# Sums of |x| due four microseconds sooner in a planned matmul-tanh-multiply kernel

## The chip, the cores and the metric

The kernel runs on one core of one Trainium2 chip. The metric is the device time of one execution in microseconds, the median over runs. The core's engines are named as in the profile: PE (TensorE, the matmuls), PEld (its weight loads), DVE (VectorE), ACT (ScalarE), POOL (GpSimd, which here only issues the loads of x), SP (SyncE, which issues transposes and stores). A name with a q is an engine's queue of instructions that only wait or issue.

## What is computed

x has 16 batches of 512 rows and 1024 columns, w1 and w2 are 1024 by 768, all float32:

```python
def reference(x, w1, w2):
    y1 = np.matmul(x, w1)
    y2 = np.matmul(x, w2)
    return (np.tanh(y1) * y2).astype(np.float32)
```

The batches are flattened to 8192 rows, which are 64 row tiles of 128.

## The kernel before

**Row tiles and triples.** Row tiles 0 to 5 (the head) and 63 (the tail) are multiplied plainly. The 57 between are taken in 19 triples: triple i has row tiles 6+3i, 7+3i and 8+3i. A triple's x is seen as six blocks (three row tiles by two halves of the 1024 columns), the weights as six blocks too (two halves of the rows by three groups of 512 columns: a column block of w1, one of w2, and the rest of both). Instead of 18 block products the kernel makes 15 (`product`, L473, four matmuls of 128x512 each), from sums of x blocks (`x_sum`, L430, on VectorE, ten for a triple, named S) and sums of weight blocks (`w_sum`, L420, eleven, made once). The products gather in eight PSUM banks; copies and seeds (`c_copy`, L479, on ScalarE) and additions (`c_add`, L488, on VectorE) combine them, `c_tanh` (L491) and `c_mul` (L496) finish a triple's outputs. 60 of PE's matmuls make up a triple.

**How x comes in.** From row tile 4 on, a row tile passes three steps. The load L (`load_x`, L380) is a DMA that POOL issues, which casts x to float16 into an xh buffer. The transpose T (`transpose`, L383; from tile 6 on) is a DMA that SP issues, from xh to an xT buffer. The sum D (`abs_x`, L386) is one ScalarE instruction over xh which adds up |x| for a later test whether float16 was good enough (`flag_1` to `flag_5`; if not, `general_path` computes all again). So an xh buffer has two readers, T and D, and the next load into it waits for both. There are few xh buffers: three at first, and one more from row tiles 15, 18 and 21 on, so six (L370 to L376, `xh_user` names whose buffer a tile takes). With six, the first load of a group of three waits for the third row tile of the triple two groups back: load 24 waits for D20 and T20, load 25 for D18 and T18, load 26 for D19 and T19. The xT buffers are three triples' worth, and a transpose waits for the last reader of the buffer's row tile nine back.

**What sets the order.** Everything is an operation of a planner (class `Planner`, L78) with an engine and cost, a due time, and what it needs. `run` goes through them like a small simulation: on each engine it takes the operation that can start first, or an urgent one that is due sooner. Operations of the kinds in `SOON` ("S" and "D", L266) are not started more than 3.0 us ahead of their due time plus the lag of PE's fixed sequence. The order that comes out is written down engine by engine, with each engine's queue strictly in that order; the chip then runs each queue in order, and each instruction waits for its own operands. The planner's times have no other effect.

PE's order of products is fixed by `PE_ORDER` (L75). The transposes of a triple are grouped (L366 to L369): the third row tile first, then the first, then the second (T23, T21, T22), followed on SP by the three stores of the triple three before (L710 to L714). The loads are issued on POOL in the order of the row tiles, each behind the one before it.

**Due times.** The sum of row tile mt has its due time from the line that the change touches (L728): `ORIGIN - 12 + 4.33 * (mt - HEAD)`, where `ORIGIN` is 35.0, `HEAD` 6, and 4.33 is about a third of a triple, which is one row tile. The sums of the weights' 16 slices (`abs_w`, L386 also) have late due times (L550) and go where ScalarE has room.

Of the kernel before, what the change touches and what calls it, by code (L numbers as in the profile page):

```python
# [77 lines left out]
class Planner:  # L78
# [13 lines left out]
    def op(self, name, engines, due, needs, fn, *args, behind=(), issued=(), chains=(), xfer=0.0, latency=None, seeds=False):  # L92


        assert name not in self.ops, name
        self.ops[name] = dict(engines=engines, due=due, needs=[n for n in needs if n], behind=[n for n in behind if n], issued=[n for n in issued if n], fn=fn, args=args,
                              chains=chains, xfer=xfer, latency=latency, seeds=seeds)
        for c in chains:
            self.chains.setdefault(c, {"left": 0, "bank": None, "end": 0.0})["left"] += 1
# [133 lines left out]
def kernel(  # L233
# [26 lines left out]
    HEAD = 6  # L260
# [49 lines left out]
    op = plan.op  # L310
# [212 lines left out]
    ORIGIN = 35.0  # L523
# [136 lines left out]
    for i in range(TRIPLES):  # L660
# [6 lines left out]
        for o in C_OPS:  # L667
# [22 lines left out]
            mt = HEAD + 3 * i + r  # L690
# [24 lines left out]
    for mt in range(4, MT):  # L715
        j = xh_user[mt]
        prev = f"L{mt - 1}" if mt > 4 else "gate"
        op(f"L{mt}", {"pool": 0.55}, None, [], load_x, mt,
           issued=[prev], behind=[f"D{j}"] + [f"{u}{j}" for u in ("T", "PT") if f"{u}{j}" in plan.ops] if j else [], xfer=1.5)
        if mt < BY_PE:  # L720
            op(f"PT{mt}", {"pe": 0.5}, None, [f"L{mt}"], transpose_pe_h, mt, ("T", mt), chains=[("T", mt)])
            op(f"T{mt}", {"dve": 0.67, "act": 0.93}, None, [f"PT{mt}"], evacuate_h, mt, ("T", mt), chains=[("T", mt)])
            plan.ops[f"PT{mt}"]["due"] = 26 + 4 * (mt - 4)
        else:
            op(f"T{mt}", {"sp": 1.35}, None, [f"L{mt}"], transpose, mt,
               issued=([f"T{t_order[t_order.index(mt) - 1]}"] if mt > BY_PE else []),
               behind=xt_readers[mt - 3 * XT_BUFS] if mt >= 3 * XT_BUFS else [], xfer=1.45, latency=2.2)
        op(f"D{mt}", {"act": 1.05}, ORIGIN - 12 + 4.33 * (mt - HEAD), [f"L{mt}"], abs_x, mt)  # L728

    op("f1", {"dve": 0.3}, None, [], flag_1, behind=[f"D{mt}" for mt in range(MT)] + [f"aw{a}{k}" for a, t, k in slices])  # L730
    op("f2", {"dve": 0.2}, None, ["f1"], flag_2)
# [116 lines left out]
```

## Time and profile before

| what | value |
|---|---|
| median of 14 runs | 309.68 us (305.81 to 316.07) |
| the profiled execution, its own time | 309.64 us |
| its span, first to last instruction | 307.8 us |
| PE busy | 294.8 us (96%), 1418 matmuls |
| DVE busy | 238.7 us (78%) |
| ACT busy | 222.4 us (72%) |
| POOL busy (issuing loads) | 33.0 us (11%) |
| sums of \|x\|, `junk<-xh` x60 | 1054 ns each |
| loads of x, median from issue to landing | 5.4 us |
| transposes, median from issue to landing | 5.1 us |
| stores of 384 KB, median from issue to landing | 6.5 us |

The page gives each engine's busy time and, in 40 slices of the span (7.7 us each), its busy share in tenths. A row of a table by stages has the stretch, its length, then busy time and number of instructions of PE, PEld, DVE, ACT and POOL, the granted PE clock, the DMA share and GB/s. A line of waits has the engine and what it wrote, the one waited for, the sum, the number of times and the longest. A line of the timeline has the start, the length, and in brackets the idle time before it with what ended it. DMA queue q0 carries POOL's loads, q1 what SP issues (transposes and stores); its lines have packets, MB, and the packets' time as a share of the 16 DMA engines' stretch.

### The profile page before, as it was taken

Reading aid. Unit: us, or ns where it says so; the run is one execution under the profiler, and the core shown is the slowest. Engines: PE = TensorE matmul, PEld = TensorE weight load, DVE = VectorE, ACT = ScalarE, POOL = GpSimd, SP = SyncE. Lnnn points to the kernel's source line nnn. Section 1 sums busy time; section 2 is a strip of 40 time slices with the busy share of each in tenths; the row PEclk is TensorE's granted clock in tenths of the full one; section 3 lists DMA queues with packets and bytes.
Section 4 is the critical chain, followed back from the end, with each engine's and each line's share of the span. In section 5 each row is a group of like instructions: output and inputs, shape, how many; then the busy total and the mean of one; then the engine's idle time right before and its main releaser. Section 6 shows DMA issues by size and latency. Waiting matters only on the chain. (4 is left out here: it accounts for less than half of the span.)

```text
span 307.8 us, 4456 instructions
## 1 busy us (share of the span) xinstructions
PE 294.8 (96%) x1418; PEld 138.9 (45%) x1418; DVE 238.7 (78%) x497; ACT 222.4 (72%) x438; POOL 33.0 (11%) x67
## 2 busy tenths in 40 slices
PE   7899999999998699999999999999999999999994
PEld 4656544444343244444444444444444444444442
DVE  1208989977975688988889897898978989779754
ACT  3779999999583567596876868668696677774641
POOL 0030111022020102020210202102020120000000
PEclk9999999999999799999999999999999999999999
DMA  7999999599999994999999899999979989996143
GB/s 276 407 399 190 161 124 145 111 144 254 184 257 135 246 244 116 227 178 275 144 250 230 185 250 151 260 187 212 279 127 275 161 237 225 183 359 270 68 174 120
DMA packets 82584, 64.79 MB, mean 210 GB/s; under 512 B 63616, under 2 KB 64128, under 8 KB 82560
## 3 DMA queue, kind: packets, MB, share of 16 engines
q1 hardware_dynamic: 73344, 47.20, 58.1%
q0 software_dynamic: 8640, 15.73, 32.9%
q10 hardware_dynamic: 576, 1.57, 1.4%
q8 instruction: 11, 0.18, 0.2%
q14 instruction: 13, 0.11, 0.1%
HBM read 39.85 MB, written 25.17 MB: 211 GB/s over the span
## 5 line engine op out<-in xcount | busy, mean ns | idle before, releaser
L473 PE MATMUL bank<-b,s 128*128 128x512 f16 x608 | 143.1, 382 | 4.6 <-DVE s L488 4.2
L473 PEld LDWEIGHTS <-s 128*128 128x128 f16 x760 | 74.8, 98 | 96.2 <-issue 8.1
L479 ACT ACTIVATE s<-bank 128x512 f32<-128x512 f32 x95 | 55.9, 595 | 42.1 <-PE bank L473 40.6
L488 DVE TENSOR_TENSOR bank<-bank,s 128x512 f32<-128x512 f32 x95 | 65.6, 694 | 26.0 <-PE bank L473 11.9
L386 ACT ACTIVATE junk<-xh 128x1024 f16<-128x1024 f16 x60 | 63.2, 1054 | 0.2
L496 DVE TENSOR_TENSOR o<-o,bank 128x256 f32<-128x256 f32 (+1 forms) x114 | 60.1, 546 | 1.0 <-ACT o L491 0.9
L473 PEld LDWEIGHTS <-xT 128*128 128x128 f16 x380 | 37.0, 98 | 46.1 <-issue 2.2
L473 PE MATMUL bank<-b,xT 128*128 128x512 f16 x228 | 55.4, 379 | 0.0
L380 POOL DMA_DIRECT2D xh<-in_x_dram x60 | 32.2, 546 | 211.0 <-ACT junk L386 204.3
L473 PE MATMUL bank<-wh,xT 128*128 128x512 f16 x152 | 39.0, 379 | 1.0 <-ACT s L479 0.7
L445 PE MATMUL bank<-wh,xT 128*128 128x512 f16 (+1 forms) x208 | 38.8, 338 | 0.8 <-ACT xT L341 0.7
L473 PE MATMUL bank<-wh,s 128*128 128x512 f16 x152 | 39.2, 380 | 0.0
L491 ACT ACTIVATE o<-bank 128x256 f32<-128x256 f32 x76 | 31.5, 436 | 10.6 <-PE bank L473 6.6
L491 ACT ACTIVATE o<-s 128x512 f32<-128x512 f32 x38 | 23.8, 627 | 12.1 <-DVE s L488 11.4
L430 DVE TENSOR_TENSOR s<-s,xT 128x512 f16<-128x512 f16 x76 | 31.6, 416 | 0.2
L445 PEld LDWEIGHTS <-xT 128*128 128x128 f16 x208 | 20.0, 98 | 17.7 <-ACT xT L341 1.4
L479 ACT ACTIVATE bank<-bank 128x512 f32<-128x512 f32 x38 | 21.2, 576 | 5.0 <-PE bank L473 2.0
L488 DVE TENSOR_TENSOR bank<-s,bank 128x512 f32<-128x512 f32 x19 | 13.2, 692 | 12.0 <-ACT o L491 10.1
L343 DVE CAST wh<-w_f 128x768 f16<-128x768 f32 x8 | 4.5, 567 | 18.9 <-DMA w_f<-in_w_dram 18.9
L430 DVE TENSOR_TENSOR s<-xT,xT 128x512 f16<-128x512 f16 x38 | 15.9, 417 | 0.0
L430 DVE TENSOR_TENSOR s<-xT,s 128x512 f16<-128x512 f16 x38 | 15.8, 416 | 0.0
L386 ACT ACTIVATE junk<-wh 128x768 f16<-128x768 f16 x16 | 13.5, 845 | 0.2
(39 smaller groups left out, 120.7 us busy)
## 6 DMA issues: line engine op xcount, KB each, us to landing
out_dram<-o SPq DMA_DIRECT2D x60, 384.0 KB, 6.5
xh<-in_x_dram POOLq DMA_DIRECT2D x60, 256.0 KB, 5.4
w_f<-in_w_dram SPq DMA_DIRECT2D x12, 384.0 KB, 8.5
x_f<-in_x_dram SPq DMA_DIRECT2D x4, 512.0 KB, 7.7
w_f<-in_w_dram ACTq DMA_DIRECT2D x4, 384.0 KB, 7.3
out_dram<-o SPq DMA_DIRECT2D x4, 256.0 KB, 2.2
xT<-xh SPq DMA_TRANSPOSE x58, 5.1
out_dram<-o SPq DMA_DIRECT2D x4, 128.0 KB, 1.8
```

The costliest lines, as they stand in the source:

```text
L343: pin(engine[e].tensor_copy(dst, src))
L380: pin(nc.gpsimd.dma_start(xhs[mt], xf[mt]))
L386: pin(nc.scalar.activation(junk[:, :src.shape[-1]], src, ACT.Abs, scale=scale, accum_out=sums[:, column:column + 1]))
L430: pin(engine[e].tensor_tensor(ss[i, v], x_operand(i, a), x_operand(i, b), OP[how]))
L445: pin(nc.tensor.matmul(b, xts[mt][:, k, :], rhs, start=first, stop=k == KO - 1, skip_group_check=True))
L473: pin(nc.tensor.matmul(place(i, dst), x_operand(i, a)[:, k, :], w_rhs(b, k), start=begins and k == 0, stop=k == KH - 1, skip_group_check=T ...
L479: pin(nc.scalar.activation(d, place(i, src), ACT.Copy, scale=float(sign)))
L488: pin(nc.vector.tensor_tensor(d, a, b, ALU.add if signs == (1, 1) else ALU.subtract))
L491: pin(nc.scalar.activation(out_tile(HEAD + 3 * i + r)[:, lo:lo + n], place(i, src)[:, :n], ACT.Tanh, scale=float(sign)))
L496: pin(nc.vector.tensor_tensor(o, o, place(i, src)[:, at:at + n], ALU.mult))
```

## The change

The due time of a row tile's sum of |x| becomes 4 us sooner, for every row tile from 4 on. Nothing else in the code differs; what the planner makes of it, on all engines, follows from that number.

```diff
@@ -725,7 +725,7 @@
             op(f"T{mt}", {"sp": 1.35}, None, [f"L{mt}"], transpose, mt,
                issued=([f"T{t_order[t_order.index(mt) - 1]}"] if mt > BY_PE else []),
                behind=xt_readers[mt - 3 * XT_BUFS] if mt >= 3 * XT_BUFS else [], xfer=1.45, latency=2.2)
-        op(f"D{mt}", {"act": 1.05}, ORIGIN - 12 + 4.33 * (mt - HEAD), [f"L{mt}"], abs_x, mt)
+        op(f"D{mt}", {"act": 1.05}, ORIGIN - 16 + 4.33 * (mt - HEAD), [f"L{mt}"], abs_x, mt)
```

## The prediction

> **What bounds the kernel now.** I read the page's slices first, then the busy time by stages, the waits, and last the records around the one gap. In the slices TensorE (PE) is full except at the start, at the end and in slices 13 and 14 (92 to 108 us); the DMA row has two holes of its own, slice 8 (54 to 62 us) and slice 16 (115 to 123).
>
> ```profile
> PE   7899999999998699999999999999999999999994
> ...
> DMA  7999999599999994999999899999979989996143
> ```
>
> By stages, 120 to 300 us holds 836 matmuls in 180 us and nothing can be gained there: PE is the limit. The loss is in 97 to 107, where PE is busy 6.0 of 10 us and its granted clock is 0.83.
>
> ```profile
> 60.00:80.00 20.00, 19.32 (x90) 8.53 (x88) 16.36 (x37) 18.53 (x39) 4.24 (x8) 1.00 0.93 179
> 80.00:97.00 17.00, 16.72 (x79) 7.43 (x77) 13.95 (x30) 11.38 (x23) 1.59 (x3) 1.00 1.11 214
> 97.00:107.00 10.00, 6.00 (x21) 2.31 (x20) 4.84 (x10) 4.26 (x8) 0.73 (x2) 0.83 1.05 214
> ...
> 120.00:300.00 180.00, 179.66 (x836) 81.65 (x835) 151.71 (x326) 129.78 (x256) 18.05 (x34) 1.00 0.93 210
> ```
>
> The waits of 90 to 110 us name it: VectorE (DVE) waits 3.7 us, once, for a transposed x; PE then waits 4.0 us for VectorE, and the load queue (POOL) had stood 11.6 us up to 88.7 and 16.0 us up to 106.3, both times behind a sum of |x| (L386).
>
> ```profile
> POOL xh L380 <- ACT junk L386: 16.0, 1, 16.0
> ...
> PE bank L473 <- DVE s L488: 4.0, 1, 4.0
> DVE s L430 <- DMA xT<-xh: 3.7, 1, 3.7
> ```
>
> ```profile
> 102.82 3.43 PE L473 MATMUL bank<-b,s 128*128 128x512 f16 x8 [4.00 <-DVE s L488]
> 106.04 1.22 PE L473 MATMUL bank<-wh,s 128*128 128x512 f16 x4
> ```
>
> The late transpose is that of row tile 21 (T21), needed by the first x sum of triple 5. It was issued at 89.23 and landed at 100.53, 11.3 us later; transposes with the rings to themselves land in 3.1 to 3.8 us (T6 to T8). What was in its way were the loads of tiles 24 to 26, issued from 88.68. Their queue is q0, the transposes' q1. While both are full, q1 hardly moves:
>
> ```profile
> q0 software_dynamic: 328, 0.61, 89.3%
> q1 hardware_dynamic: 299, 0.07, 15.1%
> ```
>
> That is 91 to 96 us: 0.61 MB of loads and 0.07 MB of transposes. So a transpose that meets loads waits them out. Earlier the rings were empty from 60 to 63 us, because the load queue stood behind a sum that ended at 61.7:
>
> ```profile
> 61.86 2.12 POOL L380 DMA_DIRECT2D xh<-in_x_dram  x4 [10.80 <-ACT junk L386]
> 74.95 2.12 POOL L380 DMA_DIRECT2D xh<-in_x_dram  x4 [10.97 <-ACT junk L386]
> 88.68 1.59 POOL L380 DMA_DIRECT2D xh<-in_x_dram  x3 [11.61 <-ACT junk L386]
> ```
>
> **What the Trainium skill says.** "DMA: Bandwidth & Descriptors", Queues, rings and completion order: each DMA engine goes round between the queues that have work, a packet at a time. The trace agrees in kind; the shares above (89 to 15) show that a turn of q0 is worth far more time. The same page, Issuing engines are not separate DMA queues: what GpSimd, SP and ScalarE issue runs on the same 16 DMA engines. The trace agrees: three loads land in 7.5 us alone (121.29 to 128.76) and took 10.6 with stores and transposes in flight (88.68 to 99.26). "TensorE: Matmul & The Clock Gate", What's actually happening: an idle PE falls to half its clock and recovers only after a busy window. Here 4.0 idle us were followed by products of 1.5 and 1.7 us instead of 0.86.
>
> **The change, part by part.** No instruction is added or removed. The order listing gives the sums of |x| about one row tile sooner in ScalarE's order, from tile 8 on, with the weight sums spread around them; a few x sums and products move on VectorE; PE's order is the same but for seven entries of the last triple; loads and transposes keep their order, some stores swap. A sum costs ScalarE about 1.15 us (1.05 and its 0.19 read, overlapping by 0.1), before as after: ScalarE's total stays.
>
> What moves is the release of the load queue, which waits in order: each group of loads stands behind the sum (and the transpose) of the buffer's last user. Followed through with durations of the trace:
> - Sum 8 now runs right after sum 7 (ends 31.9), so it ends near 33.1 instead of 37.8. Load 11 then waits only for T8 (landed 35.02): issued near 35.2 instead of 38.21, 3 us sooner; T11, loads 14 and 15 follow by 2.5 to 3.
> - Sum 14 moves ahead of two seeds, a copy, two tanh and two weight sums, to right after the copy that the trace has at 52.6 (its place there, with sums 12 and 13 ahead of it, is near 54.4). It ends near 55.6 instead of 61.5. Loads 16 to 19 start near 56 instead of 61.86, into the hole of 60 to 63.
> - Sum 17 moves ahead of a group of copies and tanh, from 73.53 to about 67: loads 20 to 23 near 68.5 instead of 74.95.
> - Sum 20 moves from 87.25 to about 81.7 (after the tanh that ends at 80.8 and one weight sum): loads 24 to 26 near 83 instead of 88.68, 5.7 us sooner. Alone they flow at 0.83 tile a us after 1.5 us of start: done near 88 to 89.5, the stores of 85 to 86.7 beside them.
> - T23, T21, T22 stand on SP behind three stores that wait for the last outputs of triple 1 (VectorE, to 84.1). They move only to 85.2, 86.5 and 89.1. With loads done at 89.5 and 1.1 us for each transpose (their rate alone in the records of 104 to 106 us), T21 lands between 92 and 95. It is needed at 96.9 in the trace's frame, or some 2 us sooner, as the order now has this x sum earlier on VectorE.
>
> So the stall goes, possibly with a rest. Its worth: the product before it starts at 97.79, the fourth after at 107.09: 9.30 us for four products of 0.863, that is 9.30 - 3.45 = 5.85, slow clock included. What is late next are small gaps, 0.18, 0.85, 0.43 and 0.38 us (at 58.4, 78.4, 91.8, 117.8), where PE waits on ScalarE or VectorE; fewer weight sums stand in a row at 68 to 71, so I count half of their 1.84, 0.9, as gone.
>
> What it may cost: sums 12 and 13 now stand ahead of the copies that products at 52.2 and 55.6 wait for. The copy at 50.63 came from a ScalarE that had idled 0.48 before it; with 1.15 us put ahead of it, it starts near 51.3 and ends near 51.8, and its product starts at 52.16: covered by 0.3, less the signal. Nothing if loads 12 and 13 have landed, up to 1 us if the sum must wait for its load with copies queued behind it, and not below nothing: I take 0.3. For a rest at T21, between nothing and 3 us, I take 0.7, since its landing spans 3 us and its need 2.
>
> Sum, against the profiled execution's own 309.64 us (span 307.8 and 1.8 around it; the median of 14 is 309.68): 309.64 - 5.85 - 0.9 + 0.3 + 0.7 = 303.9.
>
> **The rivals.** *A rest of the stall.* The loads come earlier, but with stores beside them flow at half rate, and T21 meets their last tile; half the stall stays: 303.9 + 3 = 306.9. For it: T21 is only 1.5 to 3 us sooner on SP. Against: the loads are 5.7 sooner.
> *It does nothing.* The sums were late for want of ScalarE, not by order: between 40 and 80 us it is busy 37.2 of 40. Then the loads don't move and the time is 309.6. Against: the sums pass work that isn't due, weight sums above all.
> *Slower: the collision moves to another transpose, in every triple.* After 120 us the loads (34.0 of the frame, tile 33: 134.04) meet the triple's second transpose (T31: 135.29 to 143.06, 7.8 us), which has 0.7 to 2.3 us to spare. The third sum of a triple moves by 6.3 to 6.5, so loads start near 127.6 and flow to 134.5, over T32 and T30. T30 would land near 138 instead of 135.65; its x sum starts at 139.99. Spare 2 us: covered. If two or more us go in the mixing (the loads of 91 to 97 ran at 0.45 tile a us), PE loses about 1 us in each of 13 triples: 303.9 + 13 = 317. It decides from a landing more than 4.3 us later than before; the spare of those first transposes was 1.5 to 4.3 us.
>
> **How the numbers follow.** Stall gone: 0.64, 302 to 305.5. Rest: 0.16, 305.5 to 308. Nothing: 0.07. Slower: 0.13. The range runs from all gaps gone (309.64 - 5.85 - 1.84 = 302.0) to the end of the rest's case, 308.0, and holds 0.80. This kernel's measurement tells about 0.5% (1.5 us) from no change: faster 0.80, same 0.07, slower 0.13.
>
> **What would show it.** Right: no VectorE wait over 1 us for xT<-xh between 85 and 110, PE at clock 1.00 there, loads 16, 20 and 24 issued near 56, 68.5 and 83, the DMA hole at 60 to 63 filled, and 836 matmuls per 180 us kept. Wrong: loads that move by less than 3 us, T21 in flight over 8 us, or waits of VectorE for the first transpose of a triple, again and again after 120.

## The result, and the profile after

| | before | after |
|---|---|---|
| median of all executions | 309.49 us (47, 305.36 to 316.58) | 305.34 us (10, 302.70 to 309.75) |
| profiled execution, its own time | 309.64 us | 303.98 us |
| its span | 307.8 us | 302.1 us |

The change makes the kernel faster, by 1.3%: ratio 0.987 [0.9835, 0.9905]. Ratios, here and below, are made from the executions within 1.5% of each kernel's fastest, medians from all of them, so that for a kernel whose times scatter widely the ratio flatters and the median beside it says more. The forecast, 303.9 us, was made against the profiled execution, and the profiled execution after takes 303.98. That hit is partly luck, as the sum below shows; the medians are 4.15 us apart, where 5.7 was forecast.

In the page's slices of after, PE's hole in slices 13 and 14 is gone, and the DMA row has 8 and 9 in slices 8 and 16, where it had 5 and 4. PE has a small new dent in slice 17 (121 to 128 us):

```profile
PE   8999999999999999899999999999999999999995
...
DMA  7999999899999999999999999999999999595143
```

By stages (same columns as before), 97 to 107 us has PE busy throughout, at full clock. After 120 us the last row is new: before, the same stretch held 766 matmuls and 165.00 us of PE; now 753 and 163.21. Thirteen matmuls of 0.216 us are 2.8 us lost where before had lost nothing.

```profile
60.00:80.00 20.00, 20.00 (x94) 9.05 (x93) 17.48 (x39) 17.75 (x39) 2.12 (x4) 1.00 1.09 206
80.00:97.00 17.00, 17.00 (x80) 7.73 (x79) 14.77 (x32) 12.77 (x26) 2.88 (x6) 1.00 1.19 249
97.00:107.00 10.00, 10.00 (x49) 4.49 (x47) 8.24 (x19) 8.61 (x18) 0.30 (x1) 1.00 1.11 98
```

```profile
120.00:285.00 165.00, 163.21 (x753) 73.38 (x752) 140.86 (x302) 115.51 (x232) 16.36 (x31) 1.00 1.02 215
```

The load queue (POOL, timeline of after) starts each group about six microseconds sooner than before (61.86, 74.95 and 88.68 there):

```profile
55.58 2.12 POOL L380 DMA_DIRECT2D xh<-in_x_dram  x4 [9.59 <-ACT junk L386]
68.74 2.12 POOL L380 DMA_DIRECT2D xh<-in_x_dram  x4 [11.05 <-ACT junk L386]
82.60 1.59 POOL L380 DMA_DIRECT2D xh<-in_x_dram  x3 [11.74 <-ACT junk L386]
```

The waits of 90 to 110 us name neither PE nor VectorE for a transposed x any more. The load queue still waits there, for a sum (9.6 us) and now also for transposes (10.7 us at the longest): it is released by whichever of an xh buffer's two readers comes last.

```profile
POOL xh L380 <- DMA xT<-xh: 13.1, 3, 10.7
POOL xh L380 <- ACT junk L386: 9.6, 1, 9.6
```

What the prediction did not see is on SP's queue. Before:

```profile
79.84 5.16 SPq L383 DMA_TRANSPOSE xT<-xh  x3
85.09 1.61 SPq L439 DMA_DIRECT2D out_dram<-o  x3
86.80 7.73 SPq L383 DMA_TRANSPOSE xT<-xh  x3
```

After:

```profile
74.30 5.33 SPq L383 DMA_TRANSPOSE xT<-xh  x3
79.72 1.60 SPq L439 DMA_DIRECT2D out_dram<-o  x3
81.43 9.24 SPq L383 DMA_TRANSPOSE xT<-xh  x3
```

The first row of each begins with T20, the third with T23; T21 is the second of the third row. T20 is issued when its load lands: load 20 landed at 79.82 before, at 74.28 after. T18 and T19, the three stores and then T23 and T21 follow at once, one behind the other. So the earlier loads moved T21 as well, from 89.23 to 83.80, nearly as far as they moved load 24 (88.68 to 82.60). They still meet: T21 was in flight 9.38 us (11.30 before). But it lands at 93.18 instead of 100.53, and the x sum that needs it starts at 93.43. The meeting is not avoided; it is over in time.

After 120 us VectorE waits four times for a first transpose, as that of a triple's first row tile is called here (T27, T36, T48, T54). PE loses 1.2 us after two of these waits (0.6 to 0.9 us idle, the rest in slower products) and 0.6 after a third. The timeline of after, VectorE and then PE:

```profile
121.64 0.43 DVE L430 TENSOR_TENSOR s<-xT 128x512 f16<-128x512 f16 x1 [1.29 <-DMA xT<-xh]
158.25 0.43 DVE L430 TENSOR_TENSOR s<-xT 128x512 f16<-128x512 f16 x1 [0.79 <-DMA xT<-xh]
...
210.91 0.43 DVE L430 TENSOR_TENSOR s<-xT 128x512 f16<-128x512 f16 x1 [1.66 <-DMA xT<-xh]
...
238.00 0.43 DVE L430 TENSOR_TENSOR s<-xT 128x512 f16<-128x512 f16 x1 [2.55 <-DMA xT<-xh]
```

```profile
122.73 1.02 PE L473 MATMUL bank<-b,s 128*128 128x512 f16 x4 [0.68 <-DVE bank L488]
...
239.09 2.98 PE L473 MATMUL bank<-b,s 128*128 128x512 f16 x12 [0.47 <-DVE bank L488]
```

### The profile page after: what moved, and what is told of

It is laid out like the page before. It is cut to its first block, busy times and chain, and to the rows that moved or that the text cites. A ratio compares the mean times of both kernels' runs of the same rounds, so it can differ in the third digit from the quotient of the medians.

```text
span 302.1 us, 4460 instructions
## 1 busy us (share of the span) xinstructions
PE 294.0 (97%) x1418; PEld 139.1 (46%) x1418; DVE 240.3 (80%) x497; ACT 220.0 (73%) x438; POOL 33.0 (11%) x67
## 5 line engine op out<-in xcount | busy, mean ns | idle before, releaser
L479 ACT ACTIVATE s<-bank 128x512 f32<-128x512 f32 x95 | 55.0, 596 | 35.3 <-PE bank L473 35.1
L496 DVE TENSOR_TENSOR o<-o,bank 128x256 f32<-128x256 f32 (+1 forms) x114 | 60.8, 547 | 2.6 <-ACT o L491 2.1
L491 ACT ACTIVATE o<-bank 128x256 f32<-128x256 f32 x76 | 32.3, 436 | 17.1 <-DVE bank L488 14.4
L386 ACT ACTIVATE junk<-wh 128x768 f16<-128x768 f16 x16 | 13.5, 845 | 0.2
```

The costliest lines, as they stand in the source:

```text
L386: pin(nc.scalar.activation(junk[:, :src.shape[-1]], src, ACT.Abs, scale=scale, accum_out=sums[:, column:column + 1]))
L479: pin(nc.scalar.activation(d, place(i, src), ACT.Copy, scale=float(sign)))
L491: pin(nc.scalar.activation(out_tile(HEAD + 3 * i + r)[:, lo:lo + n], place(i, src)[:, :n], ACT.Tanh, scale=float(sign)))
L496: pin(nc.vector.tensor_tensor(o, o, place(i, src)[:, at:at + n], ALU.mult))
```

## The experiments

My theory after the result: the stall at 98 us went because the load queue is released sooner by a few sums, and its price is that later loads meet first transposes. The rivals: the new order on ScalarE or VectorE did it by itself; one load's release (load 24) is enough; the gain is in the later due times. Each diff is against the kernel before, line 728, unless another is named; the number that is changed is the 12.

**Four sums only (e1).** Sums 8, 14, 17 and 20 alone are due four microseconds sooner.

```diff
-ORIGIN - 12 + 4.33 * (mt - HEAD)
+ORIGIN - (16 if mt in (8, 14, 17, 20) else 12) + 4.33 * (mt - HEAD)
```

> Only the sums of row tiles 8, 14, 17 and 20 are due 4 us sooner, the other 56 stay as before. Theory 'loads' (the gain is the earlier release of loads 11 to 26, so that T21 no longer meets loads 24 to 26): the whole gain, 303 to 305.5 us, load 24 issued near 83, no VectorE wait over 1 us for a transposed x between 85 and 110; and after 120 us the loads meet each triple's second transpose as before, so no late first transposes. Rival 'ScalarE order' (the gain is that copies no longer queue behind crowded sums): four sums of 60 bring little, 308 to 310 us.

Measured: median 307.03 us (six executions, in two groups: 302.56, 302.71 and 306.90 to 309.95), before 309.08 beside it; ratio 0.986 [0.9776, 0.9943]. The profiled execution took 302.71 us. T21 went out at 83.91 and landed at 94.24, and there is no stall at 98. Four sums of 60 take the stall away. The four slower executions were not profiled; by the median the gain is 2 us, half of the change's.

**The late sums only (e2).** Sums from row tile 24 on, which the change moves also, without the early ones.

```diff
+ORIGIN - (16 if mt > 23 else 12) + 4.33 * (mt - HEAD)
```

> The sums of row tiles 24 and later are due 4 us sooner, those up to 23 stay as before. Theory 'loads': no gain, 308.5 to 311 us, the stall near 98 to 106 with T21 in flight about 11 us is still there, and the first transposes of later triples are late as in the changed kernel. Rival 'ScalarE order': part of the gain, 305 to 308 us.

Measured: median 313.65 us (310.85 to 317.15); ratio 1.0106 [1.0048, 1.0164]. This half of the change by itself makes the kernel slower, by about 1%. Its profiled execution, 317.15 us, is the longest of the six and overstates the size: the stall at 98 is there (PE idle 4.18), and VectorE's waits for a transposed x have grown from 3.7 us, once, to the following.

```profile
DVE s L430 <- DMA xT<-xh: 14.7, 6, 3.9
```

**Loads 24 to 26 held back (e3).** All sums stay as before; before load 24 GpSimd copies one element of T22's result, so that the loads start only when T22 has landed, the last of T23, T21 and T22 on SP. This takes the meeting away from the other side.

```diff
+    def gate_x(e, mt):
+        pin(nc.gpsimd.tensor_copy(held, xts[mt][:, 0, :2].bitcast(f32)))
...
+        if mt == 24:
+            op("gate_x", {"pool": 0.2}, None, ["T22"], gate_x, 22, issued=[prev])
+            prev = "gate_x"
```

> The sums stay as before; GpSimd reads one element of row tile 22's transposed x before it issues load 24, so loads 24 to 26 wait until T22 has landed. Theory 'loads': with nothing in its way T21 lands near 93 to 95 instead of 100.5, the stall at 98 goes, 303.5 to 306 us, though these loads are issued about 8 us later than before, near 97; what follows may be late (T24 to T26), which would take 1 to 2 us back. Rival 'ScalarE order': 309 us or more, since no sum has moved.

Measured: median 303.69 us (302.61 to 311.76, seven); ratio 0.9803 [0.9752, 0.9854]. In its profiled execution (310.13 us) the loads start at 97.40, and T21, issued at 90.42, later than in any other kernel of the table below, lands 5.4 us later at 95.86.

```profile
96.89 0.18 POOL L520 COPY held<-xT 128x1 f32<-128x1 f32 x1 [20.02 <-DMA xT<-xh]
97.40 1.59 POOL L380 DMA_DIRECT2D xh<-in_x_dram  x3 [0.33 <-issue]
```

PE idles 0.2 us there instead of 4.0. By lines and tile names the trace has the instructions of ScalarE and PE in the order of before from end to end, and those of VectorE up to 103 us. So the meeting caused the stall, and the rival of a new order on ScalarE or VectorE falls. What this execution lost, it lost at 128 us: behind the loads held back T27 went out late (116.43) and met loads 30 to 32 (115.20 to 125.56), 9.9 us in flight:

```profile
128.00 5.28 PE L473 MATMUL bank<-b,s 128*128 128x512 f16 x12 [3.96 <-DVE bank L488]
```

**Loads that do not wait for sums (e4).** From row tile 6 on the sum of |x| reads xT instead of xh (the range test then sums the same values, grouped otherwise), so that an xh buffer has one reader, the transpose.

```diff
-        abs_sum(e, (xfs if mt in xfs else xhs)[mt], mt)
+        abs_sum(e, xts[mt].rearrange("p k m -> p (k m)") if mt >= BY_PE else (xfs if mt in xfs else xhs)[mt], mt)
...
-           issued=[prev], behind=[f"D{j}"] + [f"{u}{j}" for u in ("T", "PT") if f"{u}{j}" in plan.ops] if j else [], xfer=1.5)
+           issued=[prev], behind=[f"{u}{j}" for u in ("T", "PT") if f"{u}{j}" in plan.ops] if j else [], xfer=1.5)
...
-        op(f"D{mt}", {"act": 1.05}, ORIGIN - 12 + 4.33 * (mt - HEAD), [f"L{mt}"], abs_x, mt)
+        op(f"D{mt}", {"act": 1.05}, ORIGIN - 12 + 4.33 * (mt - HEAD), [f"T{mt}" if mt >= BY_PE else f"L{mt}"], abs_x, mt)
+        if mt >= BY_PE:
+            xt_readers[mt].append(f"D{mt}")
```

> From row tile 6 on the sums of |x| read the transposed x instead of the cast x, with the old due times: the same number of elements a partition, but sums over other elements, so the range test tests other sums. A load then waits for the transpose of its buffer's last user alone. Theory 'loads': load 24 is issued near 82 to 86, T21 lands by 96, 302.5 to 306 us. Rival 'ScalarE order': sums come later than before (they wait for the transposes), 309 to 313 us.

Measured: median 314.30 us (304.26 to 319.58, six), too scattered for a ratio. It is inconclusive as a test of the release, for it makes a new wait: a sum now stands on ScalarE's queue behind its transpose, and the copies behind it wait too. In the profiled execution (307.68 us) the stall at 98 is gone (T21 landed at 91.65), but PE waits 3.8 us for such copies:

```profile
PE bank L473 <- ACT s L479: 3.8, 2, 2.2
```

**Sum 20 only (e8).** The sum that releases load 24, without the three before it in the chain.

```diff
+ORIGIN - (16 if mt == 20 else 12) + 4.33 * (mt - HEAD)
```

> Only the sum of row tile 20 is due 4 us sooner. Theory 'loads': it alone releases loads 24 to 26, so these are issued near 83 instead of 88.7 and are out of the way when T21 (issued near 89 as before) flows; the stall at 98 goes or shrinks to under 2 us and the fastest executions take 303 to 305 us. Rival 'backlog' (the loads 11 to 23, all sooner, are what lets T21 in): the stall stays, 308 to 310 us.

Measured: median 310.50 us (22 executions, 305.93 to 312.51), before 309.25 (43); ratio 0.999 [0.9958, 1.0022]: no gain. Load 24 was released earlier, but only to 85.07, since it then waited for T20 (landed 84.51), the buffer's other reader. T21 did not move at all (89.20), because load 20, which heads SP's queue, did not. The earlier loads met T23, the transpose ahead of it (14.0 us in flight), and the stall grew:

```profile
103.59 3.57 PE L473 MATMUL bank<-b,s 128*128 128x512 f16 x8 [5.37 <-DVE s L488]
```

The profiled executions side by side show what decides (microseconds; the x sum is the first of triple 5, the last column the longest wait of PE between 85 and 115):

| kernel | load 20 landed | T21 issued | load 24 issued | T21 landed | x sum starts | PE idle |
|---|---|---|---|---|---|---|
| before | 79.82 | 89.23 | 88.68 | 100.53 | 100.55 | 4.0 |
| after | 74.28 | 83.80 | 82.60 | 93.18 | 93.43 | none |
| e1, four sums | 74.52 | 83.91 | 83.44 | 94.24 | 94.27 | none |
| e2, late sums | 79.44 | 89.65 | 88.63 | 100.64 | 100.67 | 4.2 |
| e3, loads held | 80.88 | 90.42 | 97.40 | 95.86 | 96.57 | 0.3 |
| e8, sum 20 | 79.41 | 89.20 | 85.07 | 101.89 | 101.92 | 5.4 |

Either T21 goes out near 84 and may take ten microseconds, or it goes out near 90 and must not meet the loads. What the first 118 us gain is also much the same each time: the product that starts at 117.83 before starts 7.4 to 8.0 us sooner in the profiled execution of every kernel with the four sums sooner (after, e1 and e5, e6, e7, e11, e12 below), 6.1 sooner in e3, 0.3 in e2, and 0.7 later in e8. The scatter between the kernels that have the gain comes after that.

**Later due times for the rest (e5, e6, e9).** If early sums help up to row tile 20 and hurt after it, the late ones should be due later than before. e5 has the four sums and, from row tile 23 on, 9 in place of 12; e6 the same with 6; e9 the 9 without the four sums.

```diff
+ORIGIN - (16 if mt in (8, 14, 17, 20) else 9 if mt > 22 else 12) + 4.33 * (mt - HEAD)
```

> Sums 8, 14, 17 and 20 are due 4 us sooner as in the four-sums kernel, and those of row tiles 23 and later 3 us later than before. Theory 'loads': after 100 us the loads of a triple are then issued about 1.3 us later against PE, after its second transpose has begun to flow; that transpose lands 3.5 to 6 us after its issue instead of 6 to 8, its x sum has 3 us or more to spare, and the executions with a second stall (near 307 to 310 us in the four-sums kernel) become rare: median 302.5 to 304.5. Rival 'chance' (the second stall has nothing to do with which transpose the loads meet): median 305 to 308 with the same two groups of times.

Measured for e5: median 301.45 us, five of six executions between 301.31 and 302.38, one of 310.51; ratio 0.9741 [0.9708, 0.9774]. In the profiled one (301.41 us) no transpose between 110 and 250 us takes over 6.4 us (12.6 in after), and PE has hardly a gap:

```profile
120.00:296.00 176.00, 175.52 (x821) 80.06 (x819) 149.17 (x317) 123.80 (x247) 16.46 (x31) 1.00 0.90 212
```

> As the kernel before it in this call, but the sums of row tiles 23 and later are due 6 us later than before. Theory 'loads': loads are issued about 4.3 us later against PE, second transposes land within 4 us; the first and third transposes of the next triple now wait for later loads and land 3 to 4 us later than in the four-sums kernel, with 1 to 3 us to spare: median 302.5 to 305. If their spare is used up, PE waits for VectorE in many triples, 308 us or more. Rival 'chance': 305 to 308 as above.

Measured for e6: median 312.07 us (21 executions from 303.54 to 316.27 and one of 446.33), slower than before beside it (309.25); the ratio, 0.9885 [0.9822, 0.9947], counts only three of them and says little. Three microseconds more were too many: VectorE waits 10.6 us for transposes and PE 3.6 us for one of ScalarE's copies.

> The sums of row tiles 23 and later are due 3 us later than before, the head's sums stay as before. Theory 'two places' (the stall at 98 us comes from the head's load releases, the later losses from where loads meet transposes): the stall at 98 to 106 stays whole, 308 to 310 us. Rival 'the later due times are the gain' of the kernel that made both changes: 302 to 305 us.

Measured for e9: median 313.85 us (22, 308.37 to 325.84); ratio 1.0044 [1.0005, 1.0082]. The stall at 98 stays, but not whole as expected (T21 issued at 89.01, landed at 99.01, PE idle 2.8): the product of 117.83 starts 3.6 us sooner than in before, though up to 104 us its ScalarE, VectorE and PE have the order of before, by lines and tile names. So the stall itself differs in size from one execution to another. Later due times are not the gain by themselves.

**The same kernels again (e7, e12), and a mixture (e11).** e7 is the changed kernel unaltered, e12 is e5 unaltered. e11 takes the change up to row tile 22 and 9 from there on.

```diff
+ORIGIN - (16 if mt < 23 else 9) + 4.33 * (mt - HEAD)
```

> The changed kernel once more, unaltered, on the same chip as the others of this call. Theory 'loads': 303 to 306 us; first transposes of some triples (in flight 8 to 13 us where they meet loads) have almost nothing to spare, and PE loses 1 to 4 us in pieces after 120 us, not at one place. Rival 'it loses nothing after 120': all executions within 1 us of each other at 302.5 to 303.5.

Measured for e7: median 306.13 us (302.39 to 312.33, six); ratio 0.9819 [0.9769, 0.9869]. The gain repeats. The profiled execution took 306.46 us, again with no stall at 98 (T21 issued 84.32, landed 92.94) and again with losses after 120, about 5.4 us this time.

> The changed kernel with the sums of row tiles 23 and later due 3 us later than before instead of 4 us sooner; the head's sums as the change has them. Theory 'two places': the change's gain without its loss after 120 us, 301 to 302.5 us in most executions, no VectorE wait for a first transpose after 120. Rival 'four sums' (the other early sums of the head cost something): 303 to 305.

Measured for e11: median 308.35 us (22 executions, 301.03 to 315.45), before 309.53 beside it; ratio 0.9793 [0.9746, 0.9841]. Only four executions took 301.03 to 301.52 us, as was expected of most; the others lost 3 to 14. In the profiled one (308.94) PE idles 5.9 us at one place, 230 us, behind T51, which was 10.7 us in flight.

> The kernel with four head sums sooner and the sums of row tiles 23 and later 3 us later than before, unaltered, once more. Its six executions lay at 301.3 to 302.4 but for one at 310.5; the like kernel with all the head's sums sooner lay between 301 and 315 over 22 executions. Theory 'chance' (both kernels lose 4 to 10 us whenever one meeting of loads and transposes sets off others, and six executions were too few to see it): a third or more of the executions lie over 304 us, median 302.5 to 308. Rival 'four sums are safer' (moving only the sums that release loads keeps clear of it): at least four in five lie under 303 us, median 301.3 to 302.

Measured for e12: median 307.25 us (302.54, 302.68, 305.70, 308.79, 310.32, 316.32), before 308.92 beside it; ratio 0.9838 [0.9768, 0.9907]. So e5's five executions within 1.1 us of each other were good luck. The profiled execution (308.79) has T21 in time as e5 had, but T43 (11.0 us in flight) and T45 (8.4) late around 190 to 203 us, with 4.7 us idle of PE behind them:

```profile
DVE s L430 <- DMA xT<-xh: 9.1, 4, 6.0
```

One and the same program thus meets or misses at a late transpose from one execution to the next. No version here beats the changed kernel reliably.

**The meeting by itself (e10).** A kernel of its own, which computes nothing of the reference and writes zeros: six rounds of six transposes alone and then six with three loads of the same size and cast started beside them. GpSimd copies one element of each result, so that the next set begins after the last has landed.

```python
for r in range(6):
    s = r % 2
    transpose(s, 0)
    transpose(s, 3)
    gate(6)
    transpose(s, 0)
    transpose(s, 3)
    load(1 - s, r + 1)
    gate(6)
```

> Computes nothing of the reference: it only casts in row tiles by threes, transposes them, and fills the output with zeros. Six times over, six transposes flow alone, then six flow while three loads of other row tiles are issued. Theory 'loads': alone each transpose takes 1.1 to 1.3 us of the rings in a row; those that meet the loads hardly move until the loads have landed, so the last of them land 4 us or more later than without loads, and while both flow the transposes' queue moves under a fifth of its own rate. Rival 'fair shares': both queues slow down by half, the last transposes land about 2 to 4 us later and the loads take twice their time.

Measured, in one execution of 201.05 us. First all transposes (L38), then all loads (L34), with the time from issue to landing:

```profile
L38 SPq DMA_TRANSPOSE xT<-xh x72: 1232/1280/4211, 5.0 to 131.4; - x72
...
DMA to landing us min/median/max: 3.1/3.4/9.7
```

```profile
DMA to landing us min/median/max: 3.8/6.3/8.4
```

Alone nearly all transposes land in 3.1 to 3.5 us. In each round the first two of the second six, issued ahead of the loads, still land so. The third and fourth meet the loads: they take 7.9 to 9.7 us and land at least 0.5 us after the last load; the fifth takes 4.8 to 5.9. The queues while both are full (18.5 to 22 us; packets, MB, share):

```profile
q0 software_dynamic: 274, 0.51, 86.0%
q1 hardware_dynamic: 292, 0.07, 14.9%
```

These are the kernel's own shares of 91 to 96 us (89 to 15) with no store and no matmul near: the loads alone do it. With the engines to itself (13 to 18 us) the transposes' queue moved 0.93 MB in 5 us. The packets say how: 274 to 292, nearly one for one. That agrees with the Trainium skill ("DMA: Bandwidth & Descriptors", Queues, rings and completion order), which says that a DMA engine goes round its queues packet by packet, if the trace's packets are those that the page means. But a load's packet carries 1.9 KB (0.51 MB by 274) and a transpose's 0.24 KB (0.07 by 292), and so of eight parts moved the loads get seven.

## Why the prediction was right, and where it was not

The lead of after over before, read as the start of the same product in the one trace minus that in the other, adds the sum up term by term:

| where (time in before) | lead afterwards, us | change | the prediction's term |
|---|---|---|---|
| first products, 38 | 0.38 | +0.38 | none |
| product at 54.7 | 0.20 | -0.18 | sums ahead of copies, -0.3 |
| small gaps, 58 to 92 | 1.81 | +1.61 | half of the gaps, +0.9 |
| the stall, 98 to 107 | 7.66 | +5.85 | +5.85 |
| gap at 118 | 8.04 | +0.38 | in the +0.9 |
| 122 to 247 | 5.10 | -2.94 | covered, nothing |
| outputs after the last products | 5.7 (span) | +0.6 | none |

- **The stall** was worth what it was said to be, 5.85 us, and it went by the chain that was followed: sum 8 ended at 32.73 (33.1 predicted), load 11 started at 35.47 (35.2), load 16 at 55.58 (56), load 20 at 68.74 (68.5), load 24 at 82.60 (83). e1 shows that these sums suffice, e8 that the last of them does not.
- **T21's landing** was predicted for 92 to 95 and came at 93.18, by two steps that were both wrong and cancelled. The loads were to be done by 89.5 and were done at 92.24, with the transposes among them. And T21 was to leave SP at 86.5, held by stores that wait for VectorE, and left at 83.80. The step that failed is "three stores that wait for the last outputs of triple 1 (VectorE, to 84.1)": what VectorE writes to 84.1 are the outputs of triple 2, and those of triple 1 were ready at 70.8. The stores stood behind T20, and T20 behind load 20; in after they go out from 79.72. The named sign of failure, T21 in flight over 8 us, came true (9.38) without the failure, because it assumed the later issue.
- **The rest at T21**, +0.7, was nothing here: 0.25 us to spare.
- **A reading of the lines**: the three loads said to land "alone" (121.29 to 128.76) had T28 in flight beside them from 122.34 and stores from 124.63. The sum does not use it.
- **Small gaps**: all of them went, 1.99 us with that of 118, not half. The fewer weight sums in a row there were the argument; that this is the cause no run isolates.
- **After 120 us** the term "covered" was wrong. The loads moved as reckoned: load 33 starts at 119.91 where PE is 8.04 us ahead, so at 127.95 in the time of before (127.6 predicted, 134.04 before), and loads 33 to 35 meet first transposes, as the rival of the other sign said. What was mis-sized is how long these then fly. T30, reckoned to land 2 us before its x sum, landed 0.4 before it (132.69; 9.33 us in flight, 4.52 before), and four others came too late. The late half alone (e2) costs about 1% of the time, the sign of that rival. Its price was wrong: 13 us, one for each triple; the profile has 2.9. The second transposes (of a triple's second row tile), which had 0.7 to 2.3 us to spare before, now mostly land with four to six, and of the first transposes only four are late enough to hold VectorE, by 0.8 to 2.6 us.

So 303.9 against 303.98 is a sum in which +0.7 at T21, +1.1 at the small gaps, +1.0 at start and end and +0.1 at the copies make up for -2.9 after 120. The losses after 120 also differ between executions: e7's profiled one lost about 5.4 us there. What remains of the scatter, which transpose is met in which execution, is not explained: nothing in the program differs between e5 and e12.

## What to carry to other kernels

Before pricing a release, follow it down every in-order queue that it feeds: here the load, then the transpose that waits for it at the head of SP, then the stores and transposes behind; the gain came through SP as much as through the load queue. Price a small-packet transfer that meets big-packet loads as if it landed after the last of them, and check the same meeting in every later period, because a shift that helps one place moves all. Where such meetings decide, six executions can mislead by 2%; run the same program again before naming a better version.

## What the runs showed of the hardware that was not expected

SP itself stands still when transposes are slow: the issue of one takes 1.28 us in the median and up to 4.2 us (e10, first line above), longest in every round for the second of those that meet the loads (3.9 to 4.2). In before the issue of T22 took 3.75 us, in e8 6.0. That delays what stands behind it by a step that no wait shows. (In after 6.2 of the 9.24 us of the row of 81.43 are issue; before T22 SP waits 2.8 us for PE to be done with an xT buffer.)

In after, 97 to 104 us, the DMA engines' records are full and hardly anything moves: 0.39 MB in 7 us, less than two row tiles' worth.

```profile
q1 hardware_dynamic: 604, 0.18, 94.4%
q0 software_dynamic: 106, 0.21, 16.7%
```

T24 and T26 take 12.55 and 14.38 us through it, and 12.2 and 13.5 in e7, but T24 3.8 to 4.8 and T26 5.6 to 6.1 in e5 and e12, whose loads 27 to 29 start at 101.76 or later instead of 93.8 to 96.8. PE did not feel it in after. What holds these packets was not tried and stays open.
